# adaLN sums finished by VectorE instead of TensorE and ScalarE, in a single-core gated short-convolution layer

## The chip, the cores and the metric

The kernel runs on one core of one Trainium2 chip. The core has a matrix engine (TensorE, PE in the profile; its weight loads stand apart as PEld), a vector engine (VectorE, DVE), a scalar engine (ScalarE, ACT), GpSimd (POOL), and SyncE (SP), which here only issues DMAs. Each engine works through its own list of instructions in order, and engines wait for each other by semaphores. The metric is the device time of one execution in microseconds (us); lower is better.

## The reference

One layer is run (DEPTH is 1) on 256 tokens of width 2048, so what is computed is:

```
h    = rmsnorm(x, norm_g)
mod  = silu(c) @ ada_w + ada_b            # c: one vector of 2048; ada_w: 2048 x 6144
shift, scale, gate = split(mod, 3)
h    = h * (1 + scale) + shift            # adaLN: one shift and one scale per feature
b_gate, c_gate, v, g = split(h @ w_in, 4) # w_in: 2048 x 16384, four parts of 4096
u    = causal depthwise conv of width 3 over (c_gate * v)
y    = (b_gate * u * silu(g)) @ w_out     # 4096 x 2048
out  = rmsnorm(x + gate * y, final_g)
```

Everything is float32. A float32 product is made on TensorE of three products of split operands: high x high, high x low and low x high.

## The kernel before

**Products.** Features lie on the 128 partitions. The 2048 features are 16 slices k of 128. `hT` holds for each k the high part `hh_` and the low part `hl_` of the modulated x for 256 tokens. The weights of `w_in` come in pieces of 1 MB (`raw_s`, 16 tiles of 128x128). ScalarE casts a piece to its high part (`hi`, in `high`, L611), VectorE subtracts to get the low part (`lo`, in `low`, L618), and TensorE runs 48 matmuls on it (L519). Here one such piece is called a block.

**Passes.** The first half of the output columns (16 of 32 tiles, "mm_s") starts before all of `hT` is known, because the 2 x 2048 columns of `ada_w` for shift and scale have to be read and summed first. `plan()` (L75) writes an order of 30 passes: each takes one of the four parts for one or two groups (chunks) of four column tiles, over a range k0..k1 of the slices that are ready by then. What a pass leaves is kept in SBUF (`acc`), and a later pass over further k takes it up again, in one of two ways. Either it is "seeded": ScalarE copies `acc` into the PSUM bank before the pass (`open_bank`, L690) and copies it back behind it (`keep`, L551). Or it isn't, and VectorE adds the bank to `acc` behind the pass (L553). The second half of the columns ("mm_b", L875) runs over all 16 slices at once, and the products with `w_out` ("mm_o", L916 to L918) come last.

**adaLN.** The slices are made ready in eight groups of two (`ADA`). The first group (k = 0, 1) is done ahead of the products in a way of its own. For each of the other seven, 8 pieces of `ada_w` (256 KB each, `at`) are loaded, and VectorE multiplies each row block by silu(c) and adds it up: two instructions of 128x512 a piece (`ada_sums`, L495 and L497), into `sums[k0]`, 128 partitions x (2 kinds x 256 columns). The sum over the 128 partitions is still to be made and has to end with features on partitions. In the kernel before, `ada_turn` has TensorE transpose four blocks of 128x128 into PSUM (`tp_g`, L504), and `ada_total` has ScalarE sum each along its free dimension (L511, four activations, each with a read of the accumulator), into `gs`. `all_scales` then makes scale and shift on VectorE (three instructions on 128x2, L656 to L658), and `features` makes two slices of `hT`: for each, ScalarE writes the high part from x (L361), VectorE overwrites x by the scaled and shifted x (L362), and VectorE subtracts the high part from that (L363).

**What sets the order.** Everything up to the eighth group is pinned to the order in which it is written out (`in_order`). The loop at L740 writes it block by block: first the cast and the low part of the block two further on (with pieces of adaLN sums in front of the low part, as far as they fit), then `get_ready`, which writes whatever is still missing of the slices that this block needs, then the products of the first chunk, and between the chunks `turn_sums`, `close_bank`, `open_bank`, `total_sums`, `all_scales`, `all_features` and more sums. How many sums fit is decided at build time by the clocks of four engines (`clock`, `spend`), which the constants on top (`SUM_US`, `LO_US`, `TOTAL_US` and so on) move on. Behind the eighth group the framework's scheduler orders the rest. On SyncE's queue the loads of weights and of `ada_w` lie in one line, and each waits there until its buffer is free.

Of the kernel before, what the change touches and what calls it, by code (L numbers as in the profile page):

```python
# [8 lines left out]
F32 = mybir.dt.float32  # L9
F32R = mybir.dt.float32r  # L10
AF = mybir.ActivationFunctionType
ALU = mybir.AluOpType

P = 128
# [36 lines left out]
RAW0 = 22.9  # L51
FIRST = 24.0
ISSUE_US = 2.0
TURN_US = 1.0
EARLY_US = 2.0
CONV_AT = 44
LOAD_US = 2.65
# [4 lines left out]
SUM_US = 1.5  # L62
STALL_US = 0.4
AHEAD_US = 3.0
ADD_US = 1.22
COPY_US = 1.03
TOTAL_US = 1.9
FEATURE_US = 0.5


# [4 lines left out]
def plan():  # L75
    steps, ready = [], [0.0] * ADA[0]
    done = {}
    pieces = [(sum(ADA[:g]), nk, i) for g, nk in enumerate(ADA) if g for i in range(4 * nk)]
    load, pe, dve, act = 0.0, 4.0, 0.0, 0.0
    burst = SLOT // P  # L80
    credit = 0.0

    def ada():
        nonlocal load, dve
        piece = pieces.pop(0)
        load = max(load, dve - AAHEAD) + ALOAD
        dve = max(dve, load + 2.0) + VPIECE
        if piece[2] == 4 * piece[1] - 1:
            ready.extend([dve + ALAG] * piece[1])
        return piece  # L90

    def products(n, need):

        nonlocal load, pe, dve, act, credit
        between = []
        load = max(load, pe - WAHEAD)
        pe = max(pe, need, load + min(n, burst) * LOAD + WLAG) + n * PRODUCTS
        for s0 in range(0, n, burst):
            sn = min(burst, n - s0)
            load += sn * LOAD  # L100
            act = max(act, load + 2.0) + sn * SBLOCK
            dve = max(dve, load + 2.0) + sn * VBLOCK
            credit += SHARE * sn / burst
            between.append([])
            while pieces and credit >= 1.0:
                credit -= 1.0
                between[-1].append(ada())
        return between

    order = [((ch, ch + 1), q) for ch in range(0, NCH, 2) for q in QUARTERS]  # L110
    new = [((0,), QUARTERS[0]), ((1,), QUARTERS[0])] + order[1:]
    while new or any(k < KT for k in done.values()):
        before = []
        hi = sum(r <= pe for r in ready)
        if new:
            p = new.pop(0)
            k0 = done[p] = 0
            if p not in order:
                del done[p]
                done[order[0]] = hi  # L120
        else:
            old = [p for p in order if done[p] < KT]
            p = old[0] if hi == KT else min(old, key=lambda p: done[p])
            k0 = done[p]
            while hi == k0:
                while len(ready) == hi:
                    before.append(ada())
                    credit -= 1.0
                pe = max(pe, ready[hi])
                hi = sum(r <= pe for r in ready)  # L130
        between = products((hi - k0) * CT * len(p[0]), ready[hi - 1])
        hows = []
        for _ in p[0]:
            seed = k0 > 0 and act < dve
            if k0 == 0:
                act += SCOPY
            elif seed:
                act += SSEED
            else:
                dve += VSUM  # L140
            hows.append(seed)
        steps.append((before, *p, k0, hi, hows, between))
        if p in order:
            done[p] = hi
    blocks = [b for step in steps for b in step[-1]][: len(PACE)]
    some = [piece for b in blocks for piece in b]
    for b, n in zip(blocks, PACE):
        b[:], some = some[:n], some[n:]
    blocks[-1].extend(some)
    return steps  # L150
# [3 lines left out]
def short_conv_layer(ctx: ExitStack, tc: tile.TileContext, x, c, norm_g, ada_w, ada_b, w_in, conv_w, w_out, final_g, out):  # L154
    nc = tc.nc
# [69 lines left out]
    pinned.enter_context(in_order())  # L225


    rows1 = const.tile([80, P], F32, tag="rows1", name="rows1")
    rows2 = const.tile([96, P], F32, tag="rows2", name="rows2")
    HX = D // 2  # L230
    GIVE = 300
# [64 lines left out]
    b_shift = vec[:, 16:32]  # L296
    b_scale1 = vec[:, 32:48]
    b_both = vec[:, 16:48].rearrange("p (s k) -> p s k", s=2)
    sh_sc = const.tile([P, KT // 2, 2], F32, tag="shsc", name="sh_sc")
    idle(1, turned[2])  # L300
    idle(2, turned[2])
# [39 lines left out]
    shift = const.tile([P, KT], F32, tag="shift", name="shift")  # L341
    scale = const.tile([P, KT], F32, tag="scale", name="scale")

    def modulate(k0, nk, sums):

        ks = slice(k0, k0 + nk)
        if nk == 1:
            nc.vector.tensor_scalar(
                out=scale[:, ks], in0=sums[1], scalar1=b_scale1[:, ks], scalar2=gT[:, ks], op0=ALU.add, op1=ALU.mult
            )  # L350
            nc.scalar.activation(shift[:, ks], sums[0], AF.Identity, bias=b_shift[:, ks])
        else:
            nc.vector.tensor_tensor(out=scale[:, ks], in0=sums[1], in1=b_scale1[:, ks], op=ALU.add)
            nc.vector.tensor_tensor(out=scale[:, ks], in0=scale[:, ks], in1=gT[:, ks], op=ALU.mult)
            nc.vector.tensor_tensor(out=shift[:, ks], in0=sums[0], in1=b_shift[:, ks], op=ALU.add)
        for k in range(k0, k0 + nk):
            features(k, scale[:, k : k + 1], shift[:, k : k + 1])

    def features(k, sc, sh):
        hf = xs[k // CT][:, k % CT, :]  # L360
        nc.scalar.activation(hh_[:, k], hf, AF.Identity, bias=sh, scale=sc)  # L361
        nc.vector.tensor_scalar(out=hf, in0=hf, scalar1=sc, scalar2=sh, op0=ALU.mult, op1=ALU.add)  # L362
        nc.vector.tensor_tensor(out=hl_[:, k], in0=hf, in1=hh_[:, k].bitcast(F32), op=ALU.subtract)  # L363

    def split(raw, n, lo_tag="lo"):

# [79 lines left out]
    first_sums(0)  # L446
    first_parts(0)
    first_sums(1)
    features(0, sh_sc[:, 0, 1:2], sh_sc[:, 0, 0:1])
    first_parts(1)  # L450
    features(1, sh_sc[:, 1, 1:2], sh_sc[:, 1, 0:1])

    def taps(ct, u, cv):

# [44 lines left out]
    def ada_turn(k0, nk):  # L499

        tp = psum.tile([P, 4, P], F32, tag="sm", name="tp_g", bufs=2)
        gv = sums[k0][:, :, 0 : nk * P]
        for o in range(2 * nk):
            nc.tensor.transpose(tp[:, o, :], gv[:, o // nk, (o % nk) * P : (o % nk + 1) * P], ident)  # L504
        return tp

    def ada_total(nk, tp):

        gs = const.tile([P, 4], F32, tag="gs", name="gs", bufs=2)
        for o in range(2 * nk):  # L510
            nc.scalar.activation(tp[:, o, :], tp[:, o, :], AF.Copy, accum_out=gs[:, o : o + 1])  # L511
        return gs[:, 0:nk], gs[:, nk : 2 * nk]

    opener = [None]
    def product(dst, hi, lo, k, i, begins, left, ends):
# [56 lines left out]
    def spend(engine, us, since=0.0):  # L572

        clock[engine] = max(clock[engine], since) + us
        return clock[engine]
# [47 lines left out]
    def sum_one():  # L623

        (k0, nk, piece), at4, at = waiting.pop(0)
        ada_sums(k0, nk, piece, at4)
        spend("dve", SUM_US, at)
        if piece == 4 * nk - 1:
            turning.append((k0, nk, clock["dve"]))
        issue()  # L630

    def sum_some(end, stall):

        while waiting and waiting[0][2] <= clock["dve"] + stall and max(clock["dve"], waiting[0][2]) + SUM_US <= end:
            sum_one()

    def turn_sums(by):

        while turning and turning[0][2] <= by:
            k0, nk, _ = turning.pop(0)  # L640
            totals.append((k0, nk, ada_turn(k0, nk)))

    def total_sums():

        while totals:
            k0, nk, tp = totals.pop(0)
            whole_sums.append((k0, nk, ada_total(nk, tp), spend("act", TOTAL_US, clock["pe"])))

    def all_scales():

        while whole_sums:
            k0, nk, (sums_shift, sums_scale), at = whole_sums.pop(0)
            while waiting and max(clock["dve"], waiting[0][2]) + SUM_US <= at + STALL_US:
                sum_one()
            ks = slice(k0, k0 + nk)
            nc.vector.tensor_tensor(out=scale[:, ks], in0=sums_scale, in1=b_scale1[:, ks], op=ALU.add)  # L656
            nc.vector.tensor_tensor(out=scale[:, ks], in0=scale[:, ks], in1=gT[:, ks], op=ALU.mult)
            nc.vector.tensor_tensor(out=shift[:, ks], in0=sums_shift, in1=b_shift[:, ks], op=ALU.add)  # L658
            spend("dve", STALL_US, at)
            scaled.append((k0, nk))  # L660

    def all_features():

        while scaled:
            k0, nk = scaled.pop(0)
            for k in range(k0, k0 + nk):
                features(k, scale[:, k : k + 1], shift[:, k : k + 1])
            ready[0] = k0 + nk
            spend("act", nk * FEATURE_US)
            spend("dve", 2 * nk * FEATURE_US)  # L670
# [69 lines left out]
    for b, (n, chs, q, k0, k1, seeds, w, s0, sk, _) in enumerate(flat):  # L740
# [20 lines left out]
                open_bank(n + 1, 1)  # L761
        adds = last and len(chs) == 2 and k0 > 0 and not seeds[0]
        sum_some(begin + us / len(chs), STALL_US)
        hi, lo = parted.pop(b)
        parted[b] = None
        for j in range(len(chs)):
# [253 lines left out]
```

## Time and profile before

| | |
|---|---|
| median of 3 runs | 912.34 us (912.31 to 913.74) |
| profiled execution | 911.95 us |
| its span, first to last instruction | 910.2 us |
| granted TensorE clock | 0.998 |
| PE busy / PEld busy | 897.1 us (99%) / 859.1 us (94%) |
| DVE busy / ACT busy | 633.5 us (70%) / 453.1 us (50%) |
| DMA | 227.63 MB, mean 250 GB/s |

Busy time of an engine says how long at least one of its instructions was running. In the page's second part each digit is a fortieth of the span (22.8 us), in tenths. The chain of waits is followed back from the last instruction, and so shows what set the end. The stretch from 0 to 24 us is preparation, 24 to 379 us are the passes of the first half (mm_s), then come the second half (mm_b, to about 728 us) and the products with `w_out`.

### The profile page before, as it was taken

The numbers are of one execution on the slowest core, as the hardware profiler recorded it, in microseconds if no ns is written. First come the engines' busy times: TensorE is split into PE (matmuls) and PEld (weight loads), VectorE is DVE, ScalarE is ACT, GpSimd is POOL, SyncE is SP. The second block draws the span as 40 slices with busy tenths as digits, with TensorE's granted clock in tenths as the row PEclk, the third lists the DMA queues.
The fourth block names the chain that finished last, engine by engine and source line by source line (L and its number), as shares of the span: only waits on it lengthen the run. The fifth ranks groups of instructions, "written<-read, shape, count | busy, mean of one in ns | idle before, by whom it ended". The sixth has DMA issues, their size and how long they took to land.

```text
span 910.2 us, 16162 instructions
## 1 busy us (share of the span) xinstructions
PE 897.1 (99%) x7045; PEld 859.1 (94%) x7045; DVE 633.5 (70%) x603; ACT 453.1 (50%) x430; POOL 1.8 (0%) x8
## 2 busy tenths in 40 slices
PE   7999999999999999999999999999999999999996
PEld 4999999999999999999999999999999988888885
DVE  5788889999656868776666666656666644555882
ACT  6788766455545746543344443344333433433333
POOL 0000000000000000000000000000000000000000
PEclk9999999999999999999999999999999999999999
DMA  9999999999565555797687778777877496665542
GB/s 310 379 382 364 313 339 347 324 325 354 198 206 190 186 190 201 246 304 240 211 262 245 237 223 269 242 237 230 256 241 240 143 358 205 201 204 188 186 139 92
DMA packets 146855, 227.63 MB, mean 250 GB/s; under 512 B 5456, under 2 KB 103904, under 8 KB 146400
## 3 DMA queue, kind: packets, MB, share of 16 engines
q1 hardware_dynamic: 146688, 226.56, 74.4%
q8 instruction: 55, 0.90, 0.4%
q14 instruction: 16, 0.13, 0.0%
q0 software_dynamic: 64, 0.02, 0.0%
q10 hardware_dynamic: 32, 0.01, 0.0%
HBM read 224.48 MB, written 2.10 MB: 249 GB/s over the span
## 4 chain that ended last, share of the span: by engine, by line
PE 95%; DMA 3%; ACT 1%; DVE 1%; SPq 0%; issue 0%; ACTq 0%
PE mm_b L519 38%; PE mm_s L519 37%; PE mm_o L917 6%; PE mm_o L918 6%; PE mm_o L916 6%; DMA at<-in_ada_w_dram 2%; DMA raw_s<-in_sc_w_in_dram 1%; DMA raw<-in_sc_w_in_dram 0%; PE tp_g L504 0%; ACT hi L611 0%; PE ps_gate L854 0%; SPq L236 0%; ACT tp_g L511 0%; DVE lo L444 0%; DVE lo L618 0%
## 5 line engine op out<-in xcount | busy, mean ns | idle before, releaser
L519 PE MATMUL mm_b<-hT,hi 128*128 128x256 f32 x2048 | 348.4, 276 | 0.0
L519 PE MATMUL mm_s<-hT,hi 128*128 128x256 f32 x2048 | 347.2, 277 | 0.7 <-DVE hT L363 0.5
L519 PEld LDWEIGHTS mm_b<-hT,hi 128*128 128x128 f32 x2048 | 308.6, 188 | 0.1
L519 PEld LDWEIGHTS mm_s<-hT,hi 128*128 128x128 f32 x2048 | 306.5, 188 | 1.5 <-DVE hT L363 0.7
L519 PE MATMUL mm_b<-hT,lo 128*128 128x256 f32 x1024 | 282.6, 276 | 0.0
L519 PE MATMUL mm_s<-hT,lo 128*128 128x256 f32 x1024 | 277.5, 276 | 0.2 <-DVE lo L618 0.2
L370 DVE TENSOR_TENSOR lo<-raw,hi 128x2048 fp32r<-128x2048 f32 x64 | 146.7, 2292 | 114.9 <-ACT hi L369 114.9
L369 ACT CAST hi<-raw 128x2048 fp32r<-128x2048 f32 x64 | 122.5, 1913 | 197.7 <-PE mm_b L519 142.5
L519 PEld LDWEIGHTS mm_b<-hT,lo 128*128 128x128 f32 x1024 | 192.2, 188 | 0.0
L519 PEld LDWEIGHTS mm_s<-hT,lo 128*128 128x128 f32 x1024 | 189.8, 188 | 0.4 <-DVE lo L618 0.4
L618 DVE TENSOR_TENSOR lo<-raw_s,hi 128x2048 fp32r<-128x2048 f32 (+1 forms) x64 | 145.5, 2273 | 49.1 <-ACT hi L611 47.7
L611 ACT CAST hi<-raw_s 128x2048 fp32r<-128x2048 f32 (+1 forms) x64 | 121.5, 1898 | 105.1 <-PE mm_s L519 82.7
L370 DVE TENSOR_TENSOR lo<-raw_o,hi 128x2048 fp32r<-128x2048 f32 x32 | 73.3, 2290 | 63.6 <-ACT hi L369 63.4
L369 ACT CAST hi<-raw_o 128x2048 fp32r<-128x2048 f32 x32 | 61.0, 1907 | 106.4 <-PE mm_o L918 84.5
L917 PE MATMUL mm_o<-lo,y 128*128 128x512 f32 x256 | 99.3, 389 | 0.0
L918 PE MATMUL mm_o<-hi,y 128*128 128x512 f32 x256 | 99.3, 389 | 0.0
L916 PE MATMUL mm_o<-hi,y 128*128 128x512 f32 x256 | 99.3, 389 | 0.0
L497 DVE SCALAR_TENSOR_TENSOR gv<-at,silu_c,gv 128x512 f32<-128x512 f32 x105 | 78.7, 750 | 2.7
L916 PEld LDWEIGHTS mm_o<-hi,y 128*128 128x128 f32 x256 | 48.1, 188 | 10.0
L917 PEld LDWEIGHTS mm_o<-lo,y 128*128 128x128 f32 x256 | 48.0, 188 | 10.0
L918 PEld LDWEIGHTS mm_o<-hi,y 128*128 128x128 f32 x256 | 48.0, 188 | 9.9
L551 ACT COPY acc<-mm_s 128x1024 f32<-128x1024 f32 x43 | 43.2, 1013 | 9.0 <-PE mm_s L519 8.7
(106 smaller groups left out, 377.6 us busy)
## 6 DMA issues: line engine op xcount, KB each, us to landing
raw<-in_sc_w_in_dram SPq DMA_DIRECT2D x64, 1024.0 KB, 6.7
raw_s<-in_sc_w_in_dram SPq DMA_DIRECT2D x63, 1024.0 KB, 6.0
raw_o<-in_sc_w_out_dram SPq DMA_DIRECT2D x32, 1024.0 KB, 5.2
at<-in_ada_w_dram SPq DMA_DIRECT2D x126, 256.0 KB, 6.7
at_g<-in_ada_w_dram SPq DMA_DIRECT2D x32, 512.0 KB, 7.5
x<-in_x_dram SPq DMA_DIRECT2D x4, 512.0 KB, 6.3
big<-in_x_dram SPq DMA_DIRECT2D x2, 1024.0 KB, 7.6
out_dram<-big SPq DMA_DIRECT2D x4, 512.0 KB, 2.9
```

What stands on the lines that cost most here:

```text
L369: nc.scalar.copy(hi[:, :n], raw[:, :n])
L370: last_low[0] = nc.vector.tensor_tensor(out=lo[:, :n], in0=raw[:, :n], in1=hi[:, :n].bitcast(F32), op=ALU.subtract)
L497: nc.vector.scalar_tensor_tensor(out=gv, in0=at4[:, i], scalar=c_k, in1=gv, op0=ALU.mult, op1=ALU.add)
L519: mm = last_mm[0] = nc.tensor.matmul(dst, w, h[:, k], start=begins and left, stop=ends, skip_group_check=True)
L551: nc.scalar.copy(acc[ch, q], bank)
L611: nc.scalar.copy(hi[:, :n], raws[b][:, :n])
L618: nc.vector.tensor_tensor(out=lo[:, :n], in0=raws.pop(b)[:, :n], in1=hi[:, :n].bitcast(F32), op=ALU.subtract)
L916: nc.tensor.matmul(po, yh, hi[:, o], start=opens, stop=False, skip_group_check=True)
L917: nc.tensor.matmul(po, yh, lo[:, o], start=False, stop=False, skip_group_check=True)
L918: nc.tensor.matmul(po, yl, hi[:, o], start=False, stop=ct == NCT - 1, skip_group_check=True)
```

## The change

In the first two of the seven groups (k0 = 2 and 4) the four TensorE transposes stay, and one VectorE sum over the whole PSUM tile takes the place of ScalarE's four sums. In the other five groups TensorE and ScalarE have no part: VectorE transposes `sums[k0]` in blocks of 32x32 into PSUM (one instruction on 128x512), sums each block's rows (one instruction, to 128x16), copies the four groups of 32 partitions side by side (four instructions on 32x16), and sums them into the four groups of 32 partitions of `gs` (four instructions). The small results lie in memory of `rows1`, which is spent by then. `features` writes scaled x to the spent memory of `sums[k0]` (of `gv0` for the first group) rather than over x. In `plan()` all passes that end beyond k = 8 are seeded. `total_sums` is called once more per block, ahead of its products, and the clocks are moved on by other constants. `modulate`, which nothing calls, is taken out.

```diff
-TURN_US = 1.0
-TOTAL_US = 1.9
+TURN_US = 0.5
+PE_TURNS = 6
+TOTAL_US = 2.95
+FOLD_US = 0.75
...
-            seed = k0 > 0 and act < dve
+            seed = k0 > 0 and (act < dve or hi > PE_TURNS + 2)
...
-    rows1 = const.tile([80, P], F32, tag="rows1", name="rows1")
+    rows1 = const.tile([P, P], F32, tag="rows1", name="rows1")
...
+    by_block = rows1[:, 0:16]
+    side = rows1[0:32, 16:80].rearrange("p (g b) -> p g b", g=4)
...
-    def features(k, sc, sh):
+    def features(k, sc, sh, whole):
         hf = xs[k // CT][:, k % CT, :]
         nc.scalar.activation(hh_[:, k], hf, AF.Identity, bias=sh, scale=sc)
-        nc.vector.tensor_scalar(out=hf, in0=hf, scalar1=sc, scalar2=sh, op0=ALU.mult, op1=ALU.add)
-        nc.vector.tensor_tensor(out=hl_[:, k], in0=hf, in1=hh_[:, k].bitcast(F32), op=ALU.subtract)
+        nc.vector.tensor_scalar(out=whole, in0=hf, scalar1=sc, scalar2=sh, op0=ALU.mult, op1=ALU.add)
+        nc.vector.tensor_tensor(out=hl_[:, k], in0=whole, in1=hh_[:, k].bitcast(F32), op=ALU.subtract)
...
-    def ada_total(nk, tp):
-
-        gs = const.tile([P, 4], F32, tag="gs", name="gs", bufs=2)
-        for o in range(2 * nk):
-            nc.scalar.activation(tp[:, o, :], tp[:, o, :], AF.Copy, accum_out=gs[:, o : o + 1])
-        return gs[:, 0:nk], gs[:, nk : 2 * nk]
+    def ada_total(k0, nk, tp):
+
+        if tp is not None:
+            gs = const.tile([P, 2, nk], F32, tag="gs", name="gs", bufs=2)
+            nc.vector.reduce_sum(gs.rearrange("p s k -> p (s k)"), tp, axis=mybir.AxisListType.X)
+            return gs[:, 0], gs[:, 1]
+        tp = psum.tile([P, 512], F32, tag="sm", name="tp_g", bufs=2)
+        nc.vector.transpose(tp, sums[k0].rearrange("p s f -> p (s f)"))
+        nc.vector.reduce_sum(by_block, tp.rearrange("p (b j) -> p b j", j=32), axis=mybir.AxisListType.X)
+        for g in range(4):
+            nc.vector.tensor_copy(out=side[:, g, :], in_=by_block[32 * g : 32 * g + 32, :])
+        gs = const.tile([P, 2, nk], F32, tag="gs", name="gs", bufs=2)
+        for g in range(4):
+            nc.vector.reduce_sum(
+                gs[32 * g : 32 * g + 32], side.rearrange("p g (s k b) -> p b s k g", s=2, k=nk)[:, g], axis=mybir.AxisListType.X
+            )
+        return gs[:, 0], gs[:, 1]
...
-        while turning and turning[0][2] <= by:
+        while turning and turning[0][0] < PE_TURNS and turning[0][2] <= by:
             k0, nk, _ = turning.pop(0)
-            totals.append((k0, nk, ada_turn(k0, nk)))
+            totals.append((k0, nk, ada_turn(k0, nk), clock["pe"]))
...
     def total_sums():
 
         while totals:
-            k0, nk, tp = totals.pop(0)
-            whole_sums.append((k0, nk, ada_total(nk, tp), spend("act", TOTAL_US, clock["pe"])))
-
-    def all_scales():
-
-        while whole_sums:
-            k0, nk, (sums_shift, sums_scale), at = whole_sums.pop(0)
+            k0, nk, tp, at = totals.pop(0)
             while waiting and max(clock["dve"], waiting[0][2]) + SUM_US <= at + STALL_US:
                 sum_one()
+            whole_sums.append((k0, nk, ada_total(k0, nk, tp)))
+            spend("dve", FOLD_US, at)
+        while turning and turning[0][0] >= PE_TURNS:
+            k0, nk, _ = turning.pop(0)
+            whole_sums.append((k0, nk, ada_total(k0, nk, None)))
+            spend("dve", TOTAL_US)
+
+    def all_scales():
+
+        while whole_sums:
+            k0, nk, (sums_shift, sums_scale) = whole_sums.pop(0)
...
-            spend("dve", STALL_US, at)
+            spend("dve", STALL_US)
...
-                features(k, scale[:, k : k + 1], shift[:, k : k + 1])
+                features(k, scale[:, k : k + 1], shift[:, k : k + 1], sums[k0][:, k - k0])
...
         sum_some(begin + us / len(chs), STALL_US)
+        total_sums()
         hi, lo = parted.pop(b)
```

More of the change, by code (lines that the diff above doesn't have):

```diff
@@ L342, in short_conv_layer @@
     scale = const.tile([P, KT], F32, tag="scale", name="scale")
[L344 to L356, printed above, removed]
-            features(k, scale[:, k : k + 1], shift[:, k : k + 1])
-    def features(k, sc, sh):
+    def features(k, sc, sh, whole):
         hf = xs[k // CT][:, k % CT, :]
         nc.scalar.activation(hh_[:, k], hf, AF.Identity, bias=sh, scale=sc)
-        nc.vector.tensor_scalar(out=hf, in0=hf, scalar1=sc, scalar2=sh, op0=ALU.mult, op1=ALU.add)
-        nc.vector.tensor_tensor(out=hl_[:, k], in0=hf, in1=hh_[:, k].bitcast(F32), op=ALU.subtract)
+        nc.vector.tensor_scalar(out=whole, in0=hf, scalar1=sc, scalar2=sh, op0=ALU.mult, op1=ALU.add)
+        nc.vector.tensor_tensor(out=hl_[:, k], in0=whole, in1=hh_[:, k].bitcast(F32), op=ALU.subtract)
     def split(raw, n, lo_tag="lo"):
@@ L448, in short_conv_layer @@
     first_sums(1)
-    features(0, sh_sc[:, 0, 1:2], sh_sc[:, 0, 0:1])
+    features(0, sh_sc[:, 0, 1:2], sh_sc[:, 0, 0:1], gv0[:, 0])
     first_parts(1)
-    features(1, sh_sc[:, 1, 1:2], sh_sc[:, 1, 0:1])
+    features(1, sh_sc[:, 1, 1:2], sh_sc[:, 1, 0:1], gv0[:, 1])
     def taps(ct, u, cv):
@@ L637, in turn_sums @@
     def turn_sums(by):
-        while turning and turning[0][2] <= by:
+        while turning and turning[0][0] < PE_TURNS and turning[0][2] <= by:
             k0, nk, _ = turning.pop(0)
-            totals.append((k0, nk, ada_turn(k0, nk)))
+            totals.append((k0, nk, ada_turn(k0, nk), clock["pe"]))
     def total_sums():
         while totals:
-            k0, nk, tp = totals.pop(0)
-            whole_sums.append((k0, nk, ada_total(nk, tp), spend("act", TOTAL_US, clock["pe"])))
+            k0, nk, tp, at = totals.pop(0)
+            while waiting and max(clock["dve"], waiting[0][2]) + SUM_US <= at + STALL_US:
+                sum_one()
+            whole_sums.append((k0, nk, ada_total(k0, nk, tp)))
[4 more added lines that the diff above has]
+            spend("dve", TOTAL_US)
     def all_scales():
         while whole_sums:
-            k0, nk, (sums_shift, sums_scale), at = whole_sums.pop(0)
-            while waiting and max(clock["dve"], waiting[0][2]) + SUM_US <= at + STALL_US:
-                sum_one()
+            k0, nk, (sums_shift, sums_scale) = whole_sums.pop(0)
             ks = slice(k0, k0 + nk)
@@ L666, in all_features @@
             for k in range(k0, k0 + nk):
-                features(k, scale[:, k : k + 1], shift[:, k : k + 1])
+                features(k, scale[:, k : k + 1], shift[:, k : k + 1], sums[k0][:, k - k0])
             ready[0] = k0 + nk
```

## The prediction, made before the changed kernel was run

> **What bounds the kernel now.** I read the page's slices first (VectorE's row here), then a table of two stretches.
>
> ```profile
> DVE  5788889999656868776666666656666644555882
> ```
> ```profile
> 24.00:120.00 96.00, 95.06 (x824) 94.08 (x823) 82.96 (x88) 75.43 (x78) 0.00 (x0) 1.00 1.01 359
> 120.00:240.00 120.00, 120.00 (x1060) 120.00 (x1059) 108.16 (x121) 68.96 (x80) 0.00 (x0) 1.00 0.93 324
> ```
>
> The columns are the stretch, its length, then busy time and instructions of PE, PEld, DVE, ACT and POOL, the granted clock, the DMA engines' share and GB/s. TensorE is never idle from 120 to 240 us and loses 0.94 us from 24 to 120. It runs at full clock (1.00), so in this stretch the end moves only if TensorE gets fewer instructions or a new wait. VectorE is next: 108.16 of 120 us, with the page's digit 9 in the slices from 136 to 227 us. ScalarE has 51 us to spare there.
>
> The chain of waits shows what the transposes cost (start, length, what ran):
>
> ```profile
> 97.09 0.61 ACT hT L361
> 97.73 0.42 DVE xs L362
> 98.18 0.44 DVE hT L363
> 98.66 24.68 PE mm_s L519 x215
> 123.34 0.44 PE tp_g L504 x4
> 123.78 27.26 PE mm_s L519 x240
> ...
> 239.55 0.44 PE tp_g L504 x4
> ...
> 275.61 103.31 PE mm_s L519 x911
> ```
>
> Each later group of transposes lies on the chain, between matmuls. And once, at 98 us, the chain leaves TensorE: the second group (k = 4, 5) came late, by way of ScalarE's cast and two VectorE steps.
>
> **Term 1: twenty transposes go.** A group takes 0.44 us on the chain. The 240 matmuls behind one take 27.26 us, where 240 at the later pace (103.31 / 911 = 0.1134) would take 27.22, so some 0.04 us more is lost on the way back. That is 0.48 a group, and 5 x 0.48 = **2.4 us**. Low bound 5 x 0.44 = 2.2, high bound 2.5 (0.5 each by the rounding of these rows). TensorE has no idle time there, so all of it counts, unless something else ends last.
>
> **Term 2: the stall at k = 4.** In TensorE's timeline the next matmul starts 0.91 us after the one before, where 0.11 is the pace: 0.80 us lost.
>
> ```profile
> 97.75 0.38 PE L519 MATMUL mm_s<-hT,hi 128*128 128x256 f32 x1
> 98.66 0.38 PE L519 MATMUL mm_s<-hT,hi 128*128 128x256 f32 x1 [0.53 <-DVE hT L363]
> ```
> ```profile
> 93.71 2.29 DVE L618 TENSOR_TENSOR lo<-raw_s,hi 128x2048 fp32r<-128x2048 f32 x1
> 96.63 0.16 DVE L656 TENSOR_TENSOR scale<-gs,vec 128x2 f32<-128x2 f32 x1 [0.63 <-ACT tp_g L511]
> 97.73 0.41 DVE L362 TENSOR_SCALAR xs<-xs,scale,shift 128x256 f32<-128x256 f32 x1 [0.67 <-ACT hT L361]
> ```
>
> This group keeps its transposes. VectorE is free at 96.00 and now sums the tile itself: 512 elements a partition from PSUM. The trace has no such sum; bounds are 0.48 (L495, 128x512, SBUF) and 1.22 (L553, 128x1024 from PSUM), and I take 0.69, the 128x512 instruction that reads PSUM (L977, all rows below). So the scale starts at about 96.7 and not 96.63: nothing gained. But L362 no longer overwrites what ScalarE still reads: its wait of 0.67 us goes, and the low part needs only the cast, which ends 97.70 (97.09 + 0.61), or 97.8 now. It starts then, and not at 98.18: **0.3 us** gained. Bounds: +0.8 if the sum costs 0.48 and all falls well; a loss of 0.2 at 1.22.
>
> **Term 3: what VectorE gets.** Rows by shape:
>
> ```profile
> L977 DVE TENSOR_TENSOR big<-mm_o,gate 128x512 f32<-128x512 f32 x6 | 3.9, 684 | 2.4 <-PE mm_o L918 2.4
> L495 DVE TENSOR_SCALAR gv<-at,silu_c 128x512 f32<-128x512 f32 x7 | 3.4, 479 | 0.0
> L553 DVE TENSOR_TENSOR acc<-mm_s,acc 128x1024 f32<-128x1024 f32 x15 | 18.3, 1220 | 5.1 <-PE mm_s L519 4.9
> L362 DVE TENSOR_SCALAR xs<-xs,scale,shift 128x256 f32<-128x256 f32 x14 | 5.7, 410 | 4.7 <-ACT hT L361 4.7
> L511 ACT ACTIVATE tp_g<-tp_g 128x128 f32<-128x128 f32 x28 | 7.4, 263 | 2.9 <-PE tp_g L504 2.3
> L690 ACT COPY mm_s<-acc 128x1024 f32<-128x1024 f32 x27 | 27.3, 1011 | 3.3 <-DVE acc L553 3.1
> ```
>
> A later turn is one block transpose and one sum of 128x512 and eight instructions of 32 partitions. The two large ones I price at 0.69 each. The small ones stand between two spacings of VectorE's timeline below, 0.08 (154.91 to 154.99, independent) and 0.19 (154.72 to 154.91, the second reads the first); I take 0.19, since they change partitions and read each other's results: 8 x 0.19 = 1.5. So T = 2.9 us a turn. Low 0.48 + 0.48 + 8 x 0.08 = 1.6; high 1.22 + 1.22 + 8 x 0.41 = 5.7, the last by L362.
>
> The Trainium skill ("VectorE: DVE Perf Modes", section "Rules for kernel authors") speaks against the step: for 128x128 it says to use TensorE where a result in PSUM will do, and VectorE's own transpose covers only 32x32 blocks. Its section "The three transpose paths" lists 311 ns for 128x128 bf16, which as an estimate makes 4 x 0.31 = 1.24 for the four, and T 3.5 instead of 2.9. No row of this trace has the operation. The rule weighs one transpose against another, while here TensorE is full and the 0.44 us it spends is on the chain.
>
> Does it fit? Passes that end beyond k = 8 lose their VectorE adds: worked through, the planner's rule keeps every k range and every piece's place, and turns 12 of the 15 unseeded chunks; three of their adds fall before 240 us. So five turns add 5 x 2.9 = 14.5 us, and 3 x 1.22 = 3.7 and five waits of 0.67 (L362) go. That leaves 7.5 us against 11.8 us idle, less the 2.4 by which the stretch gets shorter: VectorE is nearly full, but not over. Term 3 is 0, by cover of that idle time; if the cover is gone, every further microsecond a turn costs 5.
>
> Where it could show first is the group k = 8, 9:
>
> ```profile
> 150.50 2.28 DVE L618 TENSOR_TENSOR lo<-raw_s,hi 128x2048 fp32r<-128x2048 f32 x1
> 152.71 1.53 DVE L497 SCALAR_TENSOR_TENSOR gv<-at,silu_c,gv 128x512 f32<-128x512 f32 x2
> 154.72 0.16 DVE L656 TENSOR_TENSOR scale<-gs,vec 128x2 f32<-128x2 f32 x1 [0.48 <-ACT tp_g L511]
> 154.91 0.16 DVE L657 TENSOR_TENSOR scale<-scale,vec 128x2 f32<-128x2 f32 x1
> 154.99 0.16 DVE L658 TENSOR_TENSOR shift<-gs,vec 128x2 f32<-128x2 f32 x1
> ...
> 157.05 0.43 DVE L363 TENSOR_TENSOR hT<-xs,hT 128x256 fp32r<-128x256 f32 x1
> ...
> 158.53 2.28 DVE L618 TENSOR_TENSOR lo<-raw_s,hi 128x2048 fp32r<-128x2048 f32 x1
> 161.56 2.29 DVE L618 TENSOR_TENSOR lo<-raw_s,hi 128x2048 fp32r<-128x2048 f32 x1 [0.74 <-ACT hi L611]
> ```
> ```profile
> 155.18 1.09 ACT L361 ACTIVATE hT<-xs,shift,scale 128x256 fp32r<-128x256 f32 x2 [0.50 <-DVE shift L658]
> 156.18 1.90 ACT L611 CAST hi<-raw_s 128x2048 fp32r<-128x2048 f32 x1
> ```
> ```profile
> 164.96 0.39 PE L519 MATMUL mm_s<-hT,hi 128*128 128x256 f32 x2
> ```
>
> The last row is the first matmul that needs k = 8 (found by counting the 3072 mm_s matmuls by pass), and needs the low part of 158.53 to 160.81 too. ScalarE's cast at 156.18 is queued behind L361, which waits for VectorE's scales; so a late sum holds back that cast, and with it this low part. From 152.71, where VectorE is free: T, then 154.72 to 156.18 (1.46), then 156.18 to 160.81 (4.63), so the low part ends at 158.8 + T. TensorE comes at about 164.0 (two groups of transposes fewer). With T = 2.9 there are 2.3 us to spare, with one more piece (1.53) in front 0.8. It holds, narrowly.
>
> **Edits at nothing.** The seeds put 24 copies of 1.01 us on ScalarE, and 28 sums (28 x 0.26, and the reads) leave it; cover is its idle half. It is thin in one place, rival B. Writing scaled x elsewhere costs what it did in place; the memory's next writer is on VectorE too, so no new wait across engines. The first group's casts are behind a VectorE queue without such a wait, so 24 us stays. The first two turns' sums (0.69 each) lie in waits that go. No DMA is added; SyncE's line sees only later releases of buffers by VectorE.
>
> **The sum.** 911.95 profiled - 2.4 - 0.3 = 909.25. The median of the runs is 912.34, 0.4 above the profiled execution, so I predict **909.6 us**. By the skill's figure it would be the same.
>
> **Rivals.**
>
> *A, slower: the scales of k = 8 slip behind the next low parts.* How many sums precede is decided by clocks at build time, and the turn has nearly 3 us more to place. If these scales are written one block later, the low part of 158.53 goes ahead, and little is lost. If they are written two blocks later, they follow the low part of 161.56 to 163.85: T 2.9 and 154.72 to 157.48 (2.76) behind it make 169.5, against 164.0: 5.5 us lost, 909.6 + 5.5 = 915.1. The same loss comes with no slip if T is far over my value: VectorE is over-full from T = (11.8 - 2.4 + 3.7 + 3.4) / 5 = 3.3 on, and at 5.7 it is 12 us over, of which the low parts' lead covers some 6.5 (163.85 against a first use at 170.4, which is 164.96 and 48 matmuls of 0.1134): 915. For it: digit 9 in VectorE's slices. Against: adds and waits leave, and groups other than k = 8 have more lead.
>
> *B, no change: ScalarE becomes late at 300 to 324 us,* where two passes of one block follow each other.
>
> ```profile
> 300.00:324.00 24.00, 24.00 (x214) 24.00 (x213) 21.04 (x25) 17.51 (x17) 0.00 (x0) 1.00 0.62 214
> ```
>
> Six copies more are 6.1 us on 17.5: 23.6 of 24. Casts come later by up to 4 us there, about what their lead is, and up to 1.5 us may be lost: 911.1. Against: TensorE waits for nothing there now, and four adds leave VectorE.
>
> *C, no change: the loads set the pace.* The DMA engines are at 0.93 from 120 to 240 us; if bytes were the limit, the freed time would turn into waits for weights, and the whole 2.4 would go: 912.0. Against, from the waits of 120 to 240 us, where no cast waits for a load:
>
> ```profile
> ACT hi L611 <- PE mm_s L519: 43.2, 16, 3.5
> ```
>
> **How the numbers follow.** A run of this kernel can tell about 0.2% (1.8 us) from no change. The forecast has 0.60, with 908.7 to 910.4 as its own range (terms 1 and 2 at their bounds, half a microsecond of small waits). A has 0.17, B 0.15 (half of it still faster by over 0.2%), C 0.08. Faster: 0.60 + 0.07 = 0.67, less 0.04 for small slips in more places than one, 0.63; same 0.20; slower 0.17. For 8 in 10 the range runs from 908.6 past B and C to 913.2, which leaves out most of A.
>
> **What would show it.** Right: 8 transposes at L504's place, no gap in TensorE's starts between 120 and 240 us, PE busy shorter by 2.4, L553 x3, seeds x39, the gap at 98 us down to about 0.5, and a turn's ten VectorE instructions near 2.9 us. Wrong: TensorE waits on hT or a low part of 160 to 240 us (A), on a seeded bank near 310 to 320 us (B), or casts that wait for raw_s (C).

## The result, and the profile after

| | kernel before | changed kernel |
|---|---|---|
| median | 912.40 us (19 runs, 911.75 to 913.74) | 915.01 us (19 runs, 913.26 to 915.99) |
| profiled execution, its span | 911.95, 910.2 us | 913.26, 911.4 us |
| ratio | | 1.0022, 95% interval 1.0015 to 1.0029 |

The forecast was 909.6 us, faster. The changed kernel is slower, by 0.2%. Its times lie in two heaps: nine runs from 913.26 to 914.08 and ten from 915.01 to 915.99. The kernel before has one. The table's median lies in the upper heap and its profiled execution in the lower.

The changed kernel's page: first the busy times, then VectorE's row of slices.

```profile
PE 895.8 (98%) x7025; PEld 857.6 (94%) x7025; DVE 633.6 (70%) x643; ACT 465.6 (51%) x398; POOL 1.8 (0%) x8
...
DVE  5789889989956657676666666656566644555882
```

Twenty matmuls are gone (7045 to 7025) and ScalarE has 12.5 us more to do. The groups by shape show that the change does what it says. In this kernel L493 is the transpose on TensorE, L503 to L509 are VectorE's turn, L551 and L695 the copies out of and into a bank.

```profile
L551 ACT COPY acc<-mm_s 128x1024 f32<-128x1024 f32 x55 | 55.2, 1012 | 7.0 <-PE mm_s L519 6.7
...
L695 ACT COPY mm_s<-acc 128x1024 f32<-128x1024 f32 x39 | 39.6, 1017 | 1.3 <-DVE acc L553 0.7
...
L553 DVE TENSOR_TENSOR acc<-mm_s,acc 128x1024 f32<-128x1024 f32 x3 | 3.6, 1216 | 0.0
...
L503 DVE STREAM_TRANSPOSE tp_g<-gv 128x512 f32<-128x512 f32 x5 | 3.6, 718 | 0.0
L504 DVE TENSOR_REDUCE rows<-tp_g 128x16 f32<-128x512 f32 x5 | 3.5, 691 | 0.2
L509 DVE TENSOR_REDUCE gs<-rows 32x4 f32<-32x16 f32 x20 | 3.4, 170 | 0.4
L506 DVE COPY rows<-rows 32x16 f32<-32x16 f32 x20 | 3.3, 164 | 0.3
...
L493 PE MATMUL tp_g<-ident,gv 128*128 128x128 f32 x8 | 1.2, 271 | 0.0
```

And the loss has a place. The changed kernel by stretches (columns as in the prediction's table):

```profile
24.00:120.00 96.00, 95.45 (x829) 94.85 (x828) 84.31 (x91) 72.97 (x62) 0.00 (x0) 1.00 1.00 357
120.00:240.00 120.00, 120.00 (x1061) 120.00 (x1060) 111.06 (x152) 68.69 (x54) 0.00 (x0) 1.00 0.90 320
...
300.00:324.00 24.00, 21.12 (x184) 20.73 (x183) 17.18 (x21) 22.58 (x23) 0.00 (x0) 1.00 0.54 175
```

From 120 to 240 us TensorE is never idle, as before. From 300 to 324 us it is idle for 2.9 us, where before it was never idle, and ScalarE is busy for 22.58 of 24 us (17.51 before). TensorE's waits in these passes, and the two places in its timeline:

```profile
PE mm_s L519 <- ACT mm_s L695: 2.9, 2, 1.9
PE mm_s L519 <- ACT hT L350: 0.5, 1, 0.5
```
```profile
311.12 0.28 PE L519 MATMUL mm_s<-hT,lo 128*128 128x256 f32 x1
312.40 0.39 PE L519 MATMUL mm_s<-hT,hi 128*128 128x256 f32 x1 [1.00 <-ACT mm_s L695]
...
317.84 0.28 PE L519 MATMUL mm_s<-hT,lo 128*128 128x256 f32 x1
320.00 0.38 PE L519 MATMUL mm_s<-hT,hi 128*128 128x256 f32 x1 [1.88 <-ACT mm_s L695]
```

From start to start 1.28 and 2.16 us pass where 0.11 is the pace: 1.17 + 2.05 = 3.2 us lost, waiting for the copy of `acc` into a bank. ScalarE's timeline says why that copy is late. L716 is a SiLU of finished columns, with the load of its table, and L726 a cast of finished results:

```profile
303.27 1.02 ACT L551 COPY acc<-mm_s 128x1024 f32<-128x1024 f32 x1 [0.92 <-PE mm_s L519]
304.32 1.02 ACT L695 COPY mm_s<-acc 128x1024 f32<-128x1024 f32 x1
305.36 1.28 ACT L716 ACT_TABLE_LOAD   x1
306.65 1.15 ACT L716 ACTIVATE acc<-acc 128x512 f32<-128x512 f32 x2
307.71 1.90 ACT L611 CAST hi<-raw_s 128x2048 fp32r<-128x2048 f32 x1
309.51 1.92 ACT L551 COPY acc<-mm_s 128x1024 f32<-128x1024 f32 x2
311.32 1.03 ACT L695 COPY mm_s<-acc 128x1024 f32<-128x1024 f32 x1
312.26 1.16 ACT L716 ACTIVATE acc<-acc 128x512 f32<-128x512 f32 x2
313.31 1.02 ACT L695 COPY mm_s<-acc 128x1024 f32<-128x1024 f32 x1
314.26 1.92 ACT L611 CAST hi<-raw_s 128x2048 fp32r<-128x2048 f32 x1
316.06 1.02 ACT L551 COPY acc<-mm_s 128x1024 f32<-128x1024 f32 x1
316.97 1.15 ACT L726 CAST y<-acc 128x512 fp32r<-128x512 f32 x2
318.00 1.03 ACT L551 COPY acc<-mm_s 128x1024 f32<-128x1024 f32 x1
318.91 1.04 ACT L695 COPY mm_s<-acc 128x1024 f32<-128x1024 f32 x1
```

A bank that TensorE left at about 305.8 us could be emptied by ScalarE alone now, and that copy stood behind the load of a table, two SiLUs and a cast, until 309.51. Only then, behind a second copy out, comes the copy into the same bank for the next pass, 311.32 to 312.35, and TensorE goes on at 312.40. In the kernel before, VectorE emptied the bank of the same pass, as soon as TensorE had left it:

```profile
308.23 1.22 DVE L553 TENSOR_TENSOR acc<-mm_s,acc 128x1024 f32<-128x1024 f32 x1 [0.98 <-PE mm_s L519]
```

The second, longer wait comes the same way. The bank that TensorE left at about 311.3 is emptied only from 316.06 on, behind two copies into other banks, two SiLUs and a cast, and filled again from 318.91 on, behind two casts of `y` and another copy out.

How the two first traces differ can be followed matmul by matmul. At 50 us the changed kernel's is 0.2 us behind; in the first 45 us two traces of one kernel differ by more than that. The stall at k = 4 adds 0.05. The five groups without transposes bring it forward by 2.5, from 0.24 behind to 2.23 ahead. The two waits take 3.2 back, and the 24 matmuls behind each wait take 0.12 longer as well. So it ends 1.2 us later: 0.2 + 0.05 - 2.5 + 3.2 + 0.24. The upper heap is taken up with the last experiments.

### The profile page after: what moved, and what is told of

It is laid out like the page before. It is cut to its first block, busy times and chain, and to the rows that moved or that the text cites. A ratio compares the mean times of both kernels' runs of the same rounds, so it can differ in the third digit from the quotient of the medians.

```text
span 911.4 us, 16153 instructions
## 1 busy us (share of the span) xinstructions
PE 895.8 (98%) x7025; PEld 857.6 (94%) x7025; DVE 633.6 (70%) x643; ACT 465.6 (51%) x398; POOL 1.8 (0%) x8
## 4 chain that ended last, share of the span: by engine, by line
PE 94%; ACT 2%; DVE 1%; issue 1%; DMA 1%; POOL 0%; ACTq 0%; POOLq 0%
PE mm_b L519 38%; PE mm_s L519 35%; PE mm_o L924 6%; PE mm_o L922 6%; PE mm_o L923 6%; DMA rows<-in_ada_b_dram 1%; PE tp_x L289 1%; ACT hi L611 1%; ACT acc L551 1%; PE sum L374 0%; PE tp_x L343 0%; ACT mm_s L695 0%; DVE lo L618 0%; DVE gv L486 0%; ACT acc L716 0%
## 5 line engine op out<-in xcount | busy, mean ns | idle before, releaser
L551 ACT COPY acc<-mm_s 128x1024 f32<-128x1024 f32 x55 | 55.2, 1012 | 7.0 <-PE mm_s L519 6.7
```

Source lines behind the costliest of these rows:

```text
L551: nc.scalar.copy(acc[ch, q], bank)
```

## The experiments

Theory S: the loss is the late passes' seeds, on ScalarE. Rival V: it is VectorE, full from 120 to 240 us, where k = 8 and k = 12 are now barely in time. In the changed kernel's trace the last row before k = 8's first matmul and that matmul (the first of the 26th block's 48) are these, with the rows that decide when the group is done:

```profile
156.15 2.28 DVE L618 TENSOR_TENSOR lo<-raw_s,hi 128x2048 fp32r<-128x2048 f32 x1
158.35 0.72 DVE L503 STREAM_TRANSPOSE tp_g<-gv 128x512 f32<-128x512 f32 x1
...
163.27 0.43 DVE L352 TENSOR_TENSOR hT<-gv,hT 128x256 fp32r<-128x256 f32 x1
```
```profile
164.21 0.28 PE L519 MATMUL mm_s<-hT,hi 128*128 128x256 f32 x1
```

To the group's last row the lead is 0.5 us (163.70 to 164.21), against 7.5 us before (157.48 to 164.96). The turn now stands behind a low part (156.15) that came after the whole group in the kernel before (158.53).

**The old seeding rule in the changed kernel**

```diff
-            seed = k0 > 0 and (act < dve or hi > PE_TURNS + 2)
+            seed = k0 > 0 and act < dve
```

> The changed kernel with the old rule for seeding (12 chunks go back from two ScalarE copies to one VectorE add each). Theory S (the seeded passes overfill ScalarE at 300 to 324 us, and TensorE waits there 3.2 us for seeded banks): both waits vanish, and the time falls by 3.2 us or more from 915.0, to 909.9 to 911.8; the two heaps of times (913.3 to 914.1 and 915.0 to 916.0) become one. Theory V (VectorE, with 2.97 us a turn, is full from 120 to 240 us, and what is lost is lost there): three adds of 1.22 us come back into that stretch, the leads of 0.5 us (k = 8) and 0.6 us (k = 12) are used up, TensorE waits on hT by 1 to 3 us, and the time stays at 914 or more.

Measured: 916.21 us (915.15 to 916.34), ratio to before 1.0035 (1.0023 to 1.0048). Both sides were right about their part. No wait for a seeded bank is left; but with three adds back in its stretch VectorE was late for k = 12:

```profile
223.47 0.72 DVE L503 STREAM_TRANSPOSE tp_g<-gv 128x512 f32<-128x512 f32 x1
```
```profile
224.19 0.28 PE L519 MATMUL mm_s<-hT,lo 128*128 128x256 f32 x1
227.54 0.58 PE L519 MATMUL mm_s<-hT,hi 128*128 128x256 f32 x1 [3.08 <-ACT hT L350]
```

The turn stands behind one low part more than in the changed kernel and begins just before TensorE is out of work: 3.2 us lost at once, and more behind it (last section). So the seeds up to 240 us are needed.

**Seeds for passes that end at k = 10 to 14 alone**

```diff
-            seed = k0 > 0 and (act < dve or hi > PE_TURNS + 2)
+            seed = k0 > 0 and (act < dve or PE_TURNS + 2 < hi < KT)
```

> The changed kernel with the new seeding rule only for passes that end at k = 10 to 14; passes that end at 16 go by the old rule. VectorE up to 240 us is as in the changed kernel, ScalarE at 300 to 324 us as in the kernel before. S: no wait on a seeded bank, 909.9 to 911.8, one heap. V: 913 or more, with times still spread over 2 us or more.

Measured: 910.01 us (909.45 to 910.43), ratio 0.9971 (0.9959 to 0.9982); run again beside the turns on TensorE (below) 910.05 (909.93 to 910.25), ratio 0.9973 (0.9962 to 0.9984). One heap, faster than either kernel. Up to 240 us VectorE does what it does in the changed kernel; from 300 to 324 us ScalarE has room again and TensorE is never idle:

```profile
120.00:240.00 120.00, 120.00 (x1062) 120.00 (x1061) 111.14 (x151) 68.70 (x54) 0.00 (x0) 1.00 0.91 319
300.00:324.00 24.00, 24.00 (x215) 24.00 (x214) 21.05 (x23) 20.02 (x20) 0.00 (x0) 1.00 0.54 177
```

S holds; V falls as the cause of the changed kernel's loss, since VectorE's work up to 240 us is the same here.

**The new seeding rule in the kernel before, nothing else**

```diff
-            seed = k0 > 0 and act < dve
+            seed = k0 > 0 and (act < dve or hi > 8)
```

> The kernel before with nothing but the new seeding rule. S: TensorE waits some 3 us on seeded banks at 310 to 320 us; 912.4 + 3.2 = 915.6, in two heaps. V: VectorE loses adds and nothing is added to it: 912.4 or slightly less, one heap.

Measured: 915.78 us (915.58 to 916.63), ratio 1.0036 (1.0023 to 1.0048), beside 912.59 for the kernel before: 3.2 us, as S expected. The trace has the same two waits (line number of the kernel before):

```profile
PE mm_s L519 <- ACT mm_s L690: 2.9, 2, 1.9
```

The two heaps expected did not show in these five runs.

**All turns on TensorE, seeds as changed**

```diff
-PE_TURNS = 6
+PE_TURNS = 16
...
-            seed = k0 > 0 and (act < dve or hi > PE_TURNS + 2)
+            seed = k0 > 0 and (act < dve or hi > 8)
```

> The changed kernel with the transposes of all seven turns on TensorE and one VectorE sum behind them (seeding as changed). If a turn's four transposes cost 0.48 us each time: later than the changed kernel by 5 x 0.48 = 2.4, 917.4. If their place was free anyway: 915.0. V says less than 915, since VectorE loses 5 x 2.3 us.

Measured: 916.74 us (915.87 to 917.87), 1.7 us over the changed kernel's 915.01, between the two expectations. Both kernels' times are spread over 2 us, so the price of the transposes can't be read from this; it was measured again in a kernel with one heap.

**All turns on TensorE, seeds up to k = 14** (the same edit of `PE_TURNS` in the kernel with `8 < hi < KT`)

> The kernel with seeds up to k = 14 only, and the transposes of all seven turns on TensorE again, one VectorE sum behind each: the price of the transposes by themselves, in a kernel that has one heap of times. If each group of four costs 0.48 us and nothing takes it up: 910.0 + 5 x 0.48 = 912.4. If VectorE's gain of 2.3 us a turn speeds up something else: less than that.

Measured: 912.67 us (912.25 to 913.97), against 910.05 timed beside it: 2.6 us for five groups, 0.52 each. That is the first term of the prediction by itself, and nothing takes it up. The run beside it, whose times are given above:

> The kernel with seeds up to k = 14 only, once more, beside the one with its turns on TensorE: 910.0.

**The two passes of one block by the old seeding rule, all other late passes seeded**

```diff
-            seed = k0 > 0 and (act < dve or hi > PE_TURNS + 2)
+            seed = k0 > 0 and (act < dve or hi > PE_TURNS + 2 and hi - k0 > 2)
```

> The changed kernel with the new seeding rule except for the two passes of one block (k = 14 and 15 alone, at 306 to 318 us); the six longer passes that end at 16 stay seeded. If the loss lies where two passes of one block follow each other: four copies of 1.01 us leave ScalarE there, the waits on seeded banks (1.16 and 2.05) fall to under 0.5 in all, and the time is about 910.0, as with seeds up to k = 14 only. If all late seeds share in it (28 more copies in 240 to 380 us): the waits halve at best, 912 to 914.

Measured: 909.98 us (909.62 to 910.95), ratio 0.9970 (0.9957 to 0.9982), no wait on a seeded bank. The old rule still seeds the first chunk of each of the two passes; VectorE adds the second. So the late seeds in longer passes cost nothing, and the loss belongs to the two passes of one block that follow each other: there two banks are emptied and filled in the time of one block (48 x 0.1134 = 5.44 us), which is four copies to a block beside a cast.

**Scaled x written over x again** (in the kernel with seeds up to k = 14)

```diff
         hf = xs[k // CT][:, k % CT, :]
+        whole = hf
```

> The kernel with seeds up to k = 14 only, and scaled x written over x again, as before the change. Theory (the stall at k = 4 did not shrink since the low part ahead of the group came later and ate what the separate memory gives): VectorE's wait of 0.67 us for ScalarE's cast returns in each turn, and the stall at k = 4 grows from 0.99 to 1.3 to 1.7 us; elsewhere TensorE waits for nothing, or by 0.1 to 0.7 us at k = 8 and 12, whose leads were 0.5 and 0.6. Rival (the separate memory is worth nothing): 0.99 as it was, 910.0.

Measured: 910.18 us in one run, so the time says nothing at this size; the trace does. TensorE at k = 4, first with x in place, then the changed kernel:

```profile
97.65 0.28 PE L520 MATMUL mm_s<-hT,lo 128*128 128x256 f32 x1
98.41 0.38 PE L520 MATMUL mm_s<-hT,hi 128*128 128x256 f32 x1 [0.49 <-ACT hT L350]
99.32 0.39 PE L520 MATMUL mm_s<-hT,hi 128*128 128x256 f32 x1 [0.53 <-DVE hT L353]
```
```profile
97.68 0.28 PE L519 MATMUL mm_s<-hT,lo 128*128 128x256 f32 x1
98.43 0.84 PE L519 MATMUL mm_s<-hT,hi 128*128 128x256 f32 x2 [0.47 <-ACT hT L350]
```

In place the second wait is 0.91 less the pace of 0.11, 0.80 us, as in the kernel before; and the first, 0.65, is there with either. With separate memory the second is 0.35 (two matmuls in 0.84, of which the second starts 0.46 behind the first). So the separate memory is worth 0.45 us in this stall. It was eaten by the first wait, which the kernel before has at 0.14: the whole stall is 0.99 after and 0.94 before.

**Each later turn made 1.4 us longer** (in the kernel with seeds up to k = 14)

```diff
+        for _ in range(2):
-        nc.vector.transpose(tp, sums[k0].rearrange("p s f -> p (s f)"))
-        nc.vector.reduce_sum(by_block, tp.rearrange("p (b j) -> p b j", j=32), axis=mybir.AxisListType.X)
+            nc.vector.transpose(tp, sums[k0].rearrange("p s f -> p (s f)"))
+            nc.vector.reduce_sum(by_block, tp.rearrange("p (b j) -> p b j", j=32), axis=mybir.AxisListType.X)
```

> The kernel with seeds up to k = 14 only, with each later turn's block transpose and its sum made twice (0.72 + 0.69 more, T = 4.4 instead of 2.97); nothing is left out. If the leads of k = 8 (0.5 us) and k = 12 (0.6 us) are what is left of VectorE's room: TensorE waits 0.9 and 0.8 us or more there, and the time rises from 910.0 to 911.5 to 913. If VectorE still has slack that takes it up: 910.0.

Measured: 915.09 us (913.70 to 916.96), ratio 1.0028 (1.0019 to 1.0037): 5 us for 1.4 us a turn. From 120 to 300 us the trace has two waits on hT, at k = 8 and k = 12:

```profile
PE mm_s L520 <- ACT hT L350: 2.7, 2, 1.7
```

In this execution (914.01) TensorE loses 1.57 us at k = 8 and 2.17 us at k = 12, 3.7 us in all; the median is 1.1 us above it, and what that consists of was not traced. VectorE is over-full at T = 4.4, as the prediction's rival A had it (from T = 3.3 on), and carries its lateness from turn to turn: beside the trace of the kernel with seeds up to k = 14, the turn of k = 8 begins 2.0 us later (160.12 against 158.08; 0.5 of it stood from the start of the passes) and that of k = 12 4.5 us later (222.28 against 217.83). How much room is left at T = 2.97 this run doesn't say. It does show that the 0.5 us above are not the whole slack at k = 8: TensorE's first matmul there starts at 165.69, before the group's last row, which starts at 166.52.

**The changed kernel again, for its second heap**

> The changed kernel once more, for a trace of an execution from the other heap of times (915.0 to 916.0). If the heaps differ by the clock (the wait of 2 us at 318 us makes the clock gate drop now and then): a stretch with a granted clock of 0.5 behind 318 us, some 2 us longer, and all waits as in the first trace. If they differ by a wait: another wait of about 2 us, at full clock. It may fall in the lower heap, and then tells nothing of this.

This one execution took 914.92 us, span 912.9. Both waits are as in the first trace (1.16 and 2.05). But behind the second TensorE's clock is down for some 3.5 us. The same stretch, first in this trace, then in the changed kernel's first:

```profile
318.00:321.00 3.00, 1.13 (x9) 1.14 (x10) 3.00 (x6) 3.00 (x3) 0.00 (x0) 1.00 0.52 130
321.00:324.50 3.50, 3.50 (x20) 3.50 (x19) 3.50 (x4) 3.50 (x6) 0.00 (x0) 0.54 0.46 188
```
```profile
318.00:321.00 3.00, 1.12 (x10) 1.00 (x9) 3.00 (x6) 3.00 (x4) 0.00 (x0) 1.00 0.47 94
321.00:324.50 3.50, 3.50 (x33) 3.50 (x32) 3.50 (x4) 3.50 (x5) 0.00 (x0) 1.00 0.54 219
```

At a granted clock of 0.54, 20 matmuls start where 33 did: 13 x 0.113 = 1.5 us. Counted on to where the two traces keep step again, behind the end of this stretch, it is 1.7. That is most of the distance between the heaps (medians 913.5 and 915.4). That every execution of the upper heap is of this kind was not shown; one of 914.92, just under it, was traced. The executions' mean granted clocks point the same way: 0.998 on average in the lower heap and 0.996 in the upper, and 3.4 us at half clock in 912 would be 0.002. But single values overlap, 0.997 stands in both.

## Why the prediction was wrong, point by point

**The step that failed is "edits at nothing": the 24 copies that the seeds put on ScalarE,** costed at nothing by "its idle half". The runs show 3.2 us of waits in its place, from those of the copies that belong to two passes of one block. An average hid a stage. The text named the place, 300 to 324 us, counted 23.6 of 24 us for it, and gave it as rival B a chance of 0.15 and "up to 1.5 us". Behind the waits, 1.5 to 1.7 us more are lost by a lowered clock in one of two traced executions.

B's size was wrong because its mechanism was half right: it had casts come late, with their lead of several microseconds as cover. The casts came in time. Late was the bank itself: with seeding, emptying and filling a bank both need ScalarE, in order, and the copy out stood behind a table load, SiLUs and a cast that had nothing to do with it. The prediction compared ScalarE's sum of work with the length of the stretch, and didn't follow one bank through the queue.

**Term 1, the transposes, was right:** 2.4 us forecast, 2.5 between the two traces and 2.6 by itself in timed runs (912.67 against 910.05), just above its high bound of 2.5.

**Term 2, the stall at k = 4, was wrong by its whole size.** 0.3 us was forecast, 0.94 became 0.99. The wait for ScalarE's cast did go, worth 0.45. But the term took the row "VectorE is free at 96.00" of the trace before as given: in the changed kernel the low part ahead of the group ran from 94.39 to 96.68, and the sum came behind that. Why that low part came later was not followed.

**Term 3 was right.** A turn was forecast at 2.9 us and took 2.97 (0.718 + 0.691 + 4 x 0.164 + 4 x 0.170 are 2.75, and the starts are a little apart). The rule of the Trainium skill to leave 128x128 transposes to TensorE ("VectorE: DVE Perf Modes", section "Rules for kernel authors") doesn't hold for this kernel: TensorE's way costs 0.5 us a group on the path, VectorE's nothing as long as it has room. By the 311 ns that the Trainium skill has for 128x128 bf16 (the same page, section "The three transpose paths") the estimate was 1.24 for the four; the one instruction on 128x512 float32 took 0.718.

That VectorE would be "not over" is what the traces show: no wait of TensorE from 120 to 240 us. The account behind it was not right. It left 1.9 us idle (11.8 - 2.4 - 7.5), and 8.9 were idle (120 - 111.06), because only four of the five turns fall before 240 us (the fifth starts at 250.1) and six pieces of sums (62 before, 56 after) have moved behind it. Yet idle time is not room: 5.1 us of it are waits for ScalarE's casts. The forecast named the low part as the last to come at k = 8, with 0.8 to 2.3 us to spare; it was hT, since the turn had come behind that low part.

**Rival A** happened by half: the scales of k = 8 did slip behind one low part, which the text costed at little, and TensorE waited for nothing there. The slip behind two, at 5.5 us, did not happen. But its mechanism is real: with the old seeding rule k = 12 slipped behind the next low part and cost 3.2 us, and with T = 4.4 k = 8 and 12 were late. **Rival C** fell: loads don't set the pace, since the time falls by 2.3 to 2.6 us once the seeds are right (910.05 and 910.01 against 912.34 and 912.59 for the kernel before, timed beside them).

With the seeds put right, the time is 910.0, 0.4 us from the forecast. Part of that closeness is luck: Term 2's 0.3 us never came, and Term 1 gave 0.1 to 0.2 more than its price. One cover taken for granted was enough to turn the sign.

## What to carry to other kernels

Where an edit hands work to an engine that is half idle, look for the stretch where that engine is fullest and follow there one buffer through its queue: what has to be done to it, and what unrelated work stands in front. In this kernel, moving an operation off the bound engine brought its full price only when every queue that it was moved into, and every helper edit that makes room for it, was free at the moment it was needed. A rule that makes room in one stage (here the seeds, needed up to 240 us) should end with that stage.

## What the runs showed of the hardware that was not expected

In two traces here a wait of TensorE cost more than its length. Behind idle time of 2.05 us (1.17 more some 7 us earlier) the granted clock fell to 0.54 for 3.5 us in one traced execution and not in another of the same kernel, nor in the traces of two further kernels with the same two waits (the new seeding rule in the kernel before, and all turns on TensorE). With the old seeding rule, behind an idle of 3.2 us, the stretch that followed ran at half clock:

```profile
224.00:227.00 3.00, 0.46 (x5) 0.27 (x3) 2.71 (x14) 0.11 (x1) 0.00 (x0) 0.96 1.05 374
227.00:233.00 6.00, 5.46 (x24) 5.28 (x25) 3.78 (x5) 3.68 (x4) 0.00 (x0) 0.50 0.59 221
```

24 matmuls in 6 us are less than half of the usual 53. Taking 0.5 us off for the end of the wait itself, 24 fewer than the 48 of 5.46 us are 2.7 us: a wait of 3.2 us cost nearly 6. The timed runs agree: 916.21 against 910.01 with the seeds up to k = 14. The Trainium skill ("TensorE: Matmul & The Clock Gate", section "Part 1: The HAM clock gate (the "warmup" mystery)") has the clock at half after at least one idle window of about 3.4 us, and says that the windows run freely. The half clock, its length and that one execution shows it and another doesn't agree with that. But here 2.05 us of idle time was enough, and 3.2 us with the old seeding rule, both less than that window; the measurement decides.
